# Weight-block sums on GpSimd in place of adding transfers, and two early products moved ahead of the last residual

## The chip, the core and the metric

The kernel runs on one core of a Trainium2 chip. The core has five engines that work side by side: TensorE (PE, matrix products; its weight loads are listed apart as PEld), VectorE (DVE), ScalarE (ACT), GpSimd (POOL) and SyncE (SP, which here only issues transfers). Sixteen DMA engines move data between the chip's memory and the core's SBUF. The metric is the time of one execution in microseconds on the device, as the median of several runs; lower is better.

## The reference

One block of a diffusion backbone: a token mixer (gated DeltaNet, short convolution and Fourier mixing, merged by gates, then an output projection w_o) and a SwiGLU sub-layer, on 512 latent tokens of 1024 channels, all in float32. The change lies where the mixer's output projection ends and the SwiGLU's first matrix begins:

```python
x = x + g1 * mix                                   # mix = merged @ w_o
h = modulate(x, norm2_g[layer], sh2, sc2)          # RMS norm, scale, shift
a, b = split_cols(h @ w_ffn_in[layer], (D_FF, D_FF))   # D_FF = 2816
x = x + g2 * ((jax.nn.silu(a) * b) @ w_ffn_out[layer])
return rmsnorm(x, final_g)
```

## The kernel before

**Precision.** Each float32 operand is split into a rounded high part and the remainder (`split`: ACT casts the high part, L143, then DVE subtracts, L144), and a product is made of three matmuls: high x high, high x low, low x high. `prep_w` does this for weights, into two rotating buffer pairs wh/wl, or into the pair that it is given as dst.

**The output projection.** `gemm_tm` keeps eight PSUM banks (four token blocks m of 128, two halves of 512 columns) and runs over the eight row blocks of w_o; the last four, whose split weights all lie ready, are run block by block of tokens, so that the blocks end one after another. After each m the loop adds the residual (`residual`, L1008: DVE adds, ACT squares), norms it into xn, transposes it on PE (L1071) and writes h in transposed form, scaled and shifted.

**Seven products in place of eight.** h is cut in halves by channels and by tokens, and w_ffn_in into 11 column blocks g of 256, each for a and b, each cut into halves by rows. For every g a scheme with sums of blocks needs seven products of 24 matmuls (`prod`, L1108). The token sides are called B11, B21 (tokens of m = 0, 1), nB22, T1, T2, T3 (which need m = 2, 3; `sums_b` makes them) and T4. The weight sides are: v = the a-block's upper half (with B11), a12 = its lower half (with B21; these two make X, the value of a for the first 256 tokens), t = the b-block's upper plus lower half (with T1), t + v (with T2), t + v + a12 (with nB22), w = v plus the b-block's upper half (with T3), and the b-block's lower half itself (with T4).

**Early products.** B11 and B21 are done before m = 2 and 3 are, so for the first three g (`EARLY`) the products with B11 (`ahead`) and B21 (`ahead2`) are run ahead of the loop over g. In the code they stand behind the whole projection loop; `ahead` also copies the first half's sum out of PSUM (e1s).

**The sums of weights.** t and w are made by transfers: SP loads one block into t (or w) and a transfer issued by POOL adds the other to it in SBUF (`acc_w`, L1113). DVE adds v and then a12 to t (`add_w`, L1117). t lies in two buffers at the end of the tile c16 (`pre`), which are free early, w in two tiles ws. The tiles of the pool pG (ws, the third pair of split weights, T4) lie where the projection's tiles were, so nothing can be written there before those are no longer used.

**What sets the order.** A scheduler puts the instructions of each engine, and of each DMA queue, into one fixed order, by priorities: what is issued under `prio("prep")` (loads, splits and sums of weights) goes ahead of the rest as far as its model thinks it ready. Each engine then runs its list in order and waits by semaphores. SP's list of transfers is such a list too: a load that waits for a buffer holds up all loads behind it. The loads go to a pool of three buffers wf.

Of the kernel before, what the change touches and what calls it, by code (L numbers as in the profile page):

```python
# [74 lines left out]
def body(tc, I, out):  # L75
# [3 lines left out]
    with es:  # L79
# [14 lines left out]
        @contextmanager  # L94
        def prio(name):
            save = tc.cur_priority
            tc.cur_priority = prios[name]
            yield
            prios[name] = tc.cur_priority
            tc.cur_priority = save  # L100
# [874 lines left out]
        def gemm_tm(w, scale, lhs, kt, extra=(), held=2):  # L975

            ps = [[((gbank if m < 3 else tbank) if n == 0 else dbank)() for n in range(2)] for m in range(4)]

            last = held + len(extra)

            def one(k, m, wh, wl, nn=(0, 1)):
                ms = slice(128 * m, 128 * m + 128)
                for n in nn:
                    ns = slice(512 * n, 512 * n + 512)
                    mm3(ps[m][n], *lhs(k, ms), wh[:, ns], wl[:, ns], k == 0, k == kt - 1)

            for k in range(kt - last):
                wt = load_rows(w[128 * k:128 * k + 128, :], scale)
                for m in range(4):
                    one(k, m, *wt)  # L990
            dsts = list(extra) + [None] * held
            tail = [(k, load_rows(w[128 * k:128 * k + 128, :], scale, dsts[i])) for i, k in enumerate(range(kt - last, kt))]
            for m in range(4):
                for n in range(2):
                    for k, wt in tail:
                        one(k, m, *wt, nn=(n,))
                yield m, ps[m]
# [4 lines left out]
        def residual(ps, xr, m, junk):  # L1002

            sm_ = const.tile([128, 2], F32, name="n_s", tag="n_s", bufs=2)
            rs_ = const.tile([128, 1], F32, name="n_r", tag="n_r", bufs=2)
            for n in range(2):
                ns = slice(512 * n, 512 * n + 512)
                V.tensor_tensor(out=xr[:, m, ns], in0=xr[:, m, ns], in1=ps[n], op=ALU.add)  # L1008
                A.activation(out=junk[n], in_=xr[:, m, ns], func=AF.Square, accum_out=sm_[:, n:n + 1])
            V.tensor_tensor(out=rs_, in0=sm_[:, 0:1], in1=sm_[:, 1:2], op=ALU.add)  # L1010
            A.activation(out=rs_, in_=rs_, func=AF.Sqrt, scale=1.0 / 1024, bias=eps)
            V.reciprocal(out=rs_, in_=rs_)
            return rs_
# [18 lines left out]
        pre = [c16[:, a:a + 1024].rearrange("p (k j) -> p k j", k=4) for a in (2048, 3072)]  # L1032
        OB = {"B11": ob[0][:, 0], "B21": ob[0][:, 1], "nB22": ob[1][:, 0], "T3": ob[1][:, 1], "T1": ob[2][:, 0], "T2": ob[2][:, 1]}

        def split_b(f, name, js):
            split(f, OB[name][:, 0, :, js], OB[name][:, 1, :, js])

# [19 lines left out]
                                       op1=ALU.subtract)  # L1057

        for m, ps in gemm_tm(I["w_o"][0], g1b, lambda k, ms: (mh[:, k, ms], ml[:, k, ms]), 8, extra, 1):
            rs_ = residual(ps, xr, m, [xn[:, m % 2, 512 * n:512 * n + 512] for n in range(2)])  # L1060
            V.tensor_scalar(out=xn[:, m % 2], in0=xr[:, m], scalar1=rs_, scalar2=None, op0=ALU.mult)
            js = slice(128 * (m % 2), 128 * (m % 2) + 128)
            hs = []
            for k4 in range(2):
                px = dbank()
                p3 = px.rearrange("p (k j) -> p k j", k=4)
                h3 = Bf[:, 4 * k4:4 * k4 + 4, js] if m < 2 else pF.tile([128, 512], F32, name="h2f", tag=("u", "gt")[m - 2], bufs=2).rearrange("p (k j) -> p k j", k=4)
                hs.append(h3)
                for kk in range(4):
                    k = 4 * k4 + kk  # L1070
                    T.transpose(p3[:, kk], xn[:, m % 2, 128 * k:128 * k + 128], ident)  # L1071
                for kk in range(4):
                    k = 4 * k4 + kk
                    if kk % 2:
                        A.activation(out=h3[:, kk], in_=p3[:, kk], func=AF.Identity, scale=a2[:, k:k + 1], bias=sh2[:, k:k + 1])
                    else:
                        V.tensor_scalar(out=h3[:, kk], in0=p3[:, kk], scalar1=a2[:, k:k + 1], scalar2=sh2[:, k:k + 1], op0=ALU.mult, op1=ALU.add)
                if m < 2:
                    split_b(h3, ("B11", "B21")[k4], js)
            if m == 2:  # L1080
                hs2 = hs
            elif m == 3:
                sums_b(((hs2, slice(0, 128)), (hs, slice(128, 256))))
# [8 lines left out]
        e1g, e5, u2, e57, c22, c21, c12 = (tmps[:, i] for i in range(7))  # L1092
        Gq = [pG.tile([128, 2, 512], F32, name="Gq", tag=f"Gq{i}") for i in range(11)]
        ws = [pG.tile([128, 4, 256], F32, name="ws", tag=f"ws{i}") for i in range(2)]
        third = [pG.tile([128, 4, 256], F32R, name="w3", tag=f"w3{i}") for i in range(2)]
        turn = itertools.count()
        prep3 = lambda w_: prep_w(w_, dst=third if next(turn) % 3 == 2 else None)
        wfi = I["w_ffn_in"][0].rearrange("(k p) f -> p k f", p=128)
        wsrc = lambda i, half, g: wfi[:, 4 * half:4 * half + 4, 2816 * i + 256 * g:2816 * i + 256 * g + 256]

        def prod(bank, w, b, first, last):

            for q in range(2):
                o, cs = bank[:, 256 * q:256 * q + 256], slice(128 * q, 128 * q + 128)
                for kk in range(4):
                    mm = ((w[0], b[:, 0]), (w[0], b[:, 1]), (w[1], b[:, 0]))
                    for i, (l_, r_) in enumerate(mm):
                        T.matmul(o, lhsT=l_[:, kk, cs], rhs=r_[:, kk], start=first and q == kk == i == 0,  # L1108
                                 stop=last and kk == 3 and i == 2, skip_group_check=True)

        def acc_w(w, src):
            with prio("prep"):
                GP.dma_start(out=w, in_=src, accum_op=ALU.add)  # L1113

        def add_w(w, other):
            with prio("prep"):
                V.tensor_tensor(out=w, in0=w, in1=other, op=ALU.add)  # L1117

        def load_w2(src, w):
            with prio("prep"):  # L1120
                SY.dma_start(out=w, in_=src)
            return w

        def ahead(g, e):

            X = gbank()
            prod(X, prep_w(load_w(wsrc(0, 0, g))), OB["B11"], True, False)
            A.copy(out=e, in_=X)
            return X

        def ahead2(g, X):
            prod(X, prep_w(load_w(wsrc(0, 1, g))), OB["B21"], False, True)
# [1 line left out]
        e01 = stg.tile([128, 4, 256], F32, name="e01", tag="wf", bufs=3).rearrange("p a b -> p (a b)")  # L1134
        e1s = [e01[:, 0:512], e01[:, 512:1024], e1g]
        EARLY = 3
        Xs = [ahead(g, e1s[g]) for g in range(EARLY)]
        for g in range(EARLY):
            ahead2(g, Xs[g])
        V.tensor_tensor(out=Bf[:, 4:8], in0=Bf[:, 4:8], in1=Bf[:, 0:4], op=ALU.subtract)  # L1140
# [2 lines left out]
        for g in range(EARLY):  # L1143
            A.activation(out=Gq[g][:, :, 0:256], in_=q2(Xs[g]), func=AF.Silu)
        for g in range(11):
            t, w = pre[g % 2], ws[g % 2]
            load_w2(wsrc(1, 0, g), t)
            acc_w(t, wsrc(1, 1, g))
            load_w2(wsrc(0, 0, g), w)
            acc_w(w, wsrc(1, 0, g))  # L1150
            v = load_w(wsrc(0, 0, g))
            if g < EARLY:
                e1 = e1s[g]
            else:
                X, e1 = gbank(), e1g
                prod(X, prep3(v), OB["B11"], True, False)
                A.copy(out=e1, in_=X)
            bA = gbank()
            prod(bA, prep3(t), OB["T1"], True, False)
            A.copy(out=e5, in_=bA)  # L1160
            add_w(t, v)
            bD = dbank()
            prod(bD, prep3(t), OB["T2"], True, True)
            V.tensor_tensor(out=u2, in0=bD, in1=e1, op=ALU.subtract)
            bB = gbank()
            prod(bB, prep3(w), OB["T3"], True, False)
            V.tensor_tensor(out=e57, in0=bB, in1=e5, op=ALU.add)
            V.tensor_tensor(out=c22, in0=u2, in1=e57, op=ALU.add)
            a12 = load_w(wsrc(0, 1, g))
            if g >= EARLY:  # L1170
                prod(X, prep3(a12), OB["B21"], False, True)
                A.activation(out=Gq[g][:, :, 0:256], in_=q2(X), func=AF.Silu)
            add_w(t, a12)
            prod(bA, prep3(t), OB["nB22"], False, True)
            V.tensor_tensor(out=c12, in0=u2, in1=bA, op=ALU.add)
            A.activation(out=Gq[g][:, :, 256:512], in_=q2(c12), func=AF.Silu, scale=-1.0)
            prod(bB, prep3(load_w(wsrc(1, 1, g))), OB["T4"], False, True)
            V.tensor_tensor(out=c21, in0=u2, in1=bB, op=ALU.add)
            for c_, cs in ((c22, slice(256, 512)), (c21, slice(0, 256))):
                V.tensor_tensor(out=Gq[g][:, :, cs], in0=q2(c_), in1=Gq[g][:, :, cs], op=ALU.mult)  # L1180
# [38 lines left out]
```

## Time and profile before

| | us |
|---|---|
| median of 3 runs (963.09 to 968.24) | 963.99 |
| the profiled execution's own time | 965.04 |
| its span in the profile | 963.2 |
| PE busy | 939.9 |
| DVE busy | 649.3 |
| ACT busy | 467.9 |
| POOL busy | 57.2 |

The page lists the busy time of each engine, then groups of instructions as "line engine operation out<-in count, busy time, mean of one in ns, idle time before them and what ended it". A row of the timeline gives the start and the length in us, then engine, line, operation, tiles and count, and in brackets how long the engine had been idle and which instruction released it. "SPq" is SP's queue of transfers. A row of stretches gives, for each engine, its busy us and instructions, then the granted TensorE clock (1.00 is full), the mean busy share of the DMA engines and the GB/s. A row of the chain of waits gives start, length, engine, line and count.

### The profile page before, as it was taken

To read this page: it belongs to the slowest core of one execution; us is meant where nothing else is said; L and a number is where in the kernel's file an instruction comes from. 1 tells how busy PE (TensorE), PEld (TensorE's weight loads), DVE (VectorE), ACT (ScalarE), POOL (GpSimd) and SP (SyncE) were. 2 spreads that over 40 slices of the span, in tenths; PEclk is the share of its full clock that TensorE was granted. 3 is DMA by queue.
4 is the path that set the end of the run, shared out by engine and by line. 5 is a ranking of instruction groups with operands and counts; after the bars stand their busy time and mean duration, and the time that the engine had idled before them with its cause. 6 is when DMAs were issued, how large, how long until landed. Compare 5 with 4: busy or idle time off the path is not lost.

```text
span 963.2 us, 16357 instructions
## 1 busy us (share of the span) xinstructions
PE 939.9 (98%) x6660; PEld 807.7 (84%) x6660; DVE 649.3 (67%) x1002; ACT 467.9 (49%) x793; POOL 57.2 (6%) x69
## 2 busy tenths in 40 slices
PE   8999999999999999999999999799999999999997
PEld 7588887777788888888888888699999999988885
DVE  2585888378755423788874876778777777855575
ACT  5354885687673334362234336644444444422334
POOL 1002300000000000000000010112111110000000
PEclk9999999999999999999999999899999999999999
DMA  9920653521202232837774471689887774333332
GB/s 319 307 66 3 146 131 88 133 67 34 67 2 66 88 110 66 310 109 256 264 247 141 127 194 42 160 217 262 180 195 190 185 187 104 117 88 109 89 88 87
DMA packets 117434, 135.84 MB, mean 141 GB/s; under 512 B 18748, under 2 KB 104624, under 8 KB 117360
## 3 DMA queue, kind: packets, MB, share of 16 engines
q1 hardware_dynamic: 97168, 117.93, 39.2%
q0 software_dynamic: 13248, 14.98, 9.5%
q10 hardware_dynamic: 6944, 1.91, 0.8%
q8 instruction: 52, 0.85, 0.4%
q14 instruction: 22, 0.18, 0.1%
HBM read 131.02 MB, written 3.77 MB: 140 GB/s over the span
## 4 chain that ended last, share of the span: by engine, by line
PE 76%; DVE 9%; DMA 6%; ACT 6%; issue 2%; POOL 0%; SPq 0%; DVEq 0%; ACTq 0%
PE g L1108 17%; PE g L256 10%; PE g L257 10%; PE g L255 10%; PE d L256 5%; PE d L255 5%; PE d L257 5%; PE d L1108 3%; DVE wl L144 2%; DMA wm<-in_w_mod_dram 2%; DMA ws<-in_w_ffn_in_dram 1%; DVE acc L835 1%; DMA wf<-in_w_o_dram 1%; ACT wh L143 1%; ACT SJ L718 1%
## 5 line engine op out<-in xcount | busy, mean ns | idle before, releaser
L144 DVE TENSOR_TENSOR wl<-wf,wh 128x1024 fp32r<-128x1024 f32 x114 | 139.1, 1222 | 93.1 <-ACT wh L143 92.2
L143 ACT CAST wh<-wf 128x1024 fp32r<-128x1024 f32 x114 | 119.6, 1050 | 161.1 <-PE g L256 98.2
L255 PE MATMUL g<-hh,wh 128*128 128x512 f32 x368 | 145.6, 396 | 0.0
L257 PE MATMUL g<-hh,wl 128*128 128x512 f32 x368 | 145.3, 395 | 0.1
L256 PE MATMUL g<-hl,wh 128*128 128x512 f32 x368 | 145.2, 395 | 0.0
L1108 PE MATMUL g<-ob,wh 128*128 128x256 f32 x640 | 118.7, 287 | 3.8 <-ACT wh L143 3.8
L1108 PEld LDWEIGHTS g<-ob,wh 128*128 128x128 f32 x640 | 101.6, 195 | 4.5 <-ACT wh L143 4.5
L1108 PE MATMUL g<-ob,wl 128*128 128x256 f32 x320 | 91.6, 287 | 0.5 <-DVE wl L144 0.5
L257 PEld LDWEIGHTS g<-hh,wl 128*128 128x128 f32 x368 | 69.2, 188 | 14.5 <-issue 0.5
L256 PEld LDWEIGHTS g<-hl,wh 128*128 128x128 f32 x368 | 69.2, 188 | 13.6 <-issue 0.2
L255 PEld LDWEIGHTS g<-hh,wh 128*128 128x128 f32 x368 | 69.2, 188 | 13.6 <-issue 0.2
L1108 PEld LDWEIGHTS g<-ob,wl 128*128 128x128 f32 x320 | 62.3, 195 | 0.8 <-DVE wl L144 0.8
L835 DVE SCALAR_TENSOR_TENSOR acc<-wm,ct,acc 128x1024 f32<-128x1024 f32 x32 | 41.0, 1282 | 14.7 <-DMA acc<-in_b_mod_dram 7.6
L1108 PE MATMUL g<-ob,w 128*128 128x256 f32 x360 | 45.9, 283 | 0.2 <-issue 0.2
L1108 PEld LDWEIGHTS g<-ob,w 128*128 128x128 f32 x360 | 44.3, 192 | 0.4 <-issue 0.4
L143 ACT CAST gs<-Gq 128x512 fp32r<-128x512 f32 x22 | 13.4, 622 | 63.5 <-PE d L256 63.5
L143 ACT CAST wh<-c 128x1024 fp32r<-128x1024 f32 x21 | 22.0, 1048 | 37.0 <-DVE c L1117 19.5
L144 DVE TENSOR_TENSOR gs<-Gq,gs 128x512 fp32r<-128x512 f32 x22 | 15.0, 690 | 29.1 <-ACT gs L143 29.1
L154 DVE TENSOR_TENSOR wf<-wf,g2b 128x1024 f32<-128x1024 f32 x22 | 26.9, 1222 | 8.5 <-DMA wf<-in_w_ffn_out_dram 8.5
L255 PE MATMUL d<-wh,gs 128*128 128x512 f32 x80 | 31.1, 389 | 0.0
L257 PE MATMUL d<-wh,gs 128*128 128x512 f32 x80 | 31.1, 389 | 0.0
L256 PE MATMUL d<-wl,gs 128*128 128x512 f32 x80 | 31.1, 389 | 0.0
(481 smaller groups left out, 2078.3 us busy)
## 6 DMA issues: line engine op xcount, KB each, us to landing
wm<-in_w_mod_dram SPq DMA_DIRECT2D x48, 512.0 KB, 5.7
wf<-in_w_ffn_in_dram SPq DMA_DIRECT2D x39, 512.0 KB, 4.8
wf<-in_w_in_dram SPq DMA_DIRECT2D x31, 512.0 KB, 3.8
wf<-in_w_gate_dram SPq DMA_DIRECT2D x24, 512.0 KB, 3.8
wf<-in_w_ffn_out_dram SPq DMA_DIRECT2D x22, 512.0 KB, 3.6
c<-in_w_ffn_in_dram SPq DMA_DIRECT2D x11, 512.0 KB, 6.3
c<-in_w_ffn_in_dram POOLq DMA_DIRECT2D x11, 512.0 KB, 6.6
ws<-in_w_ffn_in_dram SPq DMA_DIRECT2D x11, 512.0 KB, 3.8
```

The lines of the kernel that those rows point to most:

```text
L143: A.copy(out=hi, in_=f)
L144: V.tensor_tensor(out=lo, in0=f, in1=hi.bitcast(F32), op=ALU.subtract)
L154: V.tensor_tensor(out=w, in0=w, in1=scale, op=ALU.mult)
L255: T.matmul(ps, lhsT=lh, rhs=rh, start=start, stop=False)
L256: T.matmul(ps, lhsT=lh, rhs=rl, start=False, stop=False)
L257: T.matmul(ps, lhsT=ll, rhs=rh, start=False, stop=stop)
L718: A.activation(out=S[:, u ^ par, h], in_=S[:, u ^ par, h], func=AF.Copy, scale=eGl[:, u, c_:c_ + 1])
L835: V.scalar_tensor_tensor(out=acc, in0=w, scalar=ct[:, k, 0:1], in1=acc, op0=ALU.mult, op1=ALU.add)
L1108: T.matmul(o, lhsT=l_[:, kk, cs], rhs=r_[:, kk], start=first and q == kk == i == 0, stop=last and kk == 3 and i == 2, skip_group_check=True)
```

## The change

`prod`, `wfi` and `wsrc` are moved up unchanged. Inside the projection's loop, at m = 3 and ahead of that block's residual, the products of g = 0 and 1 with B11 are now issued; the split weights of g = 1 go into the place of nB22, which is filled later. The copies to e1s and the third early product stay behind the loop. A further tile low (one of its own, two in c16's first half) holds the b-block's lower half, which also serves the T4 product, so it is loaded once. ws holds the b-block's upper half; GpSimd writes t = ws + low, then w = ws + v in place.

```diff
         for m, ps in gemm_tm(I["w_o"][0], g1b, lambda k, ms: (mh[:, k, ms], ml[:, k, ms]), 8, extra, 1):
+            if m == 3:
+
+                Xs = [gbank() for _ in range(2)]
+                for g, dst in enumerate((None, (OB["nB22"][:, 0], OB["nB22"][:, 1]))):
+                    prod(Xs[g], prep_w(load_w(wsrc(0, 0, g)), dst=dst), OB["B11"], True, False)
             rs_ = residual(ps, xr, m, [xn[:, m % 2, 512 * n:512 * n + 512] for n in range(2)])
...
+        low = [pG.tile([128, 4, 256], F32, name="low", tag="low")]
+        low += [c16[:, a:a + 1024].rearrange("p (k j) -> p k j", k=4) for a in (0, 1024)]
...
-        def acc_w(w, src):
+        def sum_w(out, a, b, eng):
             with prio("prep"):
-                GP.dma_start(out=w, in_=src, accum_op=ALU.add)
-
-        def add_w(w, other):
-            with prio("prep"):
-                V.tensor_tensor(out=w, in0=w, in1=other, op=ALU.add)
+                eng.tensor_tensor(out=out, in0=a, in1=b, op=ALU.add)
...
-        Xs = [ahead(g, e1s[g]) for g in range(EARLY)]
+        for g in range(2):
+            A.copy(out=e1s[g], in_=Xs[g])
+        Xs.append(gbank())
+        prod(Xs[2], prep_w(load_w(wsrc(0, 0, 2))), OB["B11"], True, False)
+        A.copy(out=e1s[2], in_=Xs[2])
...
-            t, w = pre[g % 2], ws[g % 2]
-            load_w2(wsrc(1, 0, g), t)
-            acc_w(t, wsrc(1, 1, g))
-            load_w2(wsrc(0, 0, g), w)
-            acc_w(w, wsrc(1, 0, g))
+            t, w, a22 = pre[g % 2], ws[g % 2], low[g % 3]
+            load_w2(wsrc(1, 0, g), w)
+            load_w2(wsrc(1, 1, g), a22)
             v = load_w(wsrc(0, 0, g))
+            sum_w(t, w, a22, GP)
+            sum_w(w, w, v, GP)
...
-            add_w(t, v)
+            sum_w(t, t, v, V)
...
-            add_w(t, a12)
+            sum_w(t, t, a12, V)
             prod(bA, prep3(t), OB["nB22"], False, True)
...
-            prod(bB, prep3(load_w(wsrc(1, 1, g))), OB["T4"], False, True)
+            prod(bB, prep3(a22), OB["T4"], False, True)
```

On PE, at the end of the projection, before: the first early product (PSUM bank g_5735, weights wh_5738 and wl_5739), the transposes of m = 3 (from xn), then the second (g_5767).

```order
L1108 MATMUL g_5735<-ob_5311,wh_5738 128x256 x2
L1108 MATMUL g_5735<-ob_5311,wl_5739 128x256
L1071 MATMUL d_5669<-cp_82,xn_5310 128x128 x4
L1071 MATMUL d_5679<-cp_82,xn_5310 128x128 x4
L1108 MATMUL g_5767<-ob_5311,wh_5770 128x256 x2
L1108 MATMUL g_5767<-ob_5311,wl_5771 128x256
```

And at the same place now, with the second product's split weights in ob_5312 (nB22):

```order
L1045 MATMUL g_5659<-ob_5311,wh_5663 128x256 x2
L1045 MATMUL g_5659<-ob_5311,wl_5664 128x256
L1045 MATMUL g_5660<-ob_5311,ob_5312 128x256 x24
L1089 MATMUL d_5729<-cp_82,xn_5310 128x128 x4
L1089 MATMUL d_5739<-cp_82,xn_5310 128x128 x4
L1045 MATMUL g_5798<-ob_5311,wh_5801 128x256 x2
L1045 MATMUL g_5798<-ob_5311,wl_5802 128x256
```

The second product's 24 matmuls have moved from behind the transposes to ahead of them; the third (g_5798) now follows the transposes directly.

On SP's queue from the last w_o loads on, before: the two loads of t for g = 0 and 1 (c16) stand ahead of four w_o loads, and the first two of w (ws) behind five loads for early products.

```order
L139 DMA wf_5416<-in_w_o_dram 128x1024
L1121 DMA c16_5314<-in_w_ffn_in_dram 128x4x256 x2
L139 DMA wf_5447<-in_w_o_dram 128x1024
L139 DMA wf_5452<-in_w_o_dram 128x1024
L139 DMA wf_5457<-in_w_o_dram 128x1024
L139 DMA wf_5462<-in_w_o_dram 128x1024
L139 DMA wf_5736<-in_w_ffn_in_dram 128x4x256
L139 DMA wf_5768<-in_w_ffn_in_dram 128x4x256
L139 DMA wf_5800<-in_w_ffn_in_dram 128x4x256
L139 DMA wf_5831<-in_w_ffn_in_dram 128x4x256
L139 DMA wf_5861<-in_w_ffn_in_dram 128x4x256
L1121 DMA ws_5730<-in_w_ffn_in_dram 128x4x256
```

Now, from the last w_o load on:

```order
L139 DMA wf_5462<-in_w_o_dram 128x1024
L139 DMA wf_5661<-in_w_ffn_in_dram 128x4x256
L139 DMA wf_5691<-in_w_ffn_in_dram 128x4x256
L139 DMA wf_5799<-in_w_ffn_in_dram 128x4x256
L139 DMA wf_5830<-in_w_ffn_in_dram 128x4x256
L139 DMA wf_5860<-in_w_ffn_in_dram 128x4x256
L139 DMA wf_5890<-in_w_ffn_in_dram 128x4x256
L139 DMA wf_5928<-in_w_ffn_in_dram 128x4x256
L1125 DMA ws_5790<-in_w_ffn_in_dram 128x4x256
L1125 DMA low_5792<-in_w_ffn_in_dram 128x4x256
L139 DMA wf_6022<-in_w_ffn_in_dram 128x4x256
L1125 DMA ws_5791<-in_w_ffn_in_dram 128x4x256
```

The loads of t are gone from ahead of the w_o loads; the first two blocks that t is made of (ws_5790, low_5792) stand behind six loads for early products and the load of v (wf_5928). By the semaphores of this list, wf_5860 waits for the split of wf_5799, wf_5928 for the split of wf_5860, and ws_5790 for DVE's last subtraction in `sums_b`.

On POOL's queue behind the last small transfer of the mixer, before:

```order
L830 DMA acc_4842<-in_b_mod_dram 1x16x64
L1113 DMA c16_5314<-in_w_ffn_in_dram 128x4x256 x2
L1113 DMA ws_5730<-in_w_ffn_in_dram 128x4x256
L1113 DMA ws_5731<-in_w_ffn_in_dram 128x4x256
L1113 DMA ws_5730<-in_w_ffn_in_dram 128x4x256
```

and now:

```order
L830 DMA acc_4842<-in_b_mod_dram 1x16x64
L1121 ISA
L1121 TENSOR_TENSOR c16_5314<-ws_5790,low_5792 128x1024
L1121 TENSOR_TENSOR ws_5790<-ws_5790,wf_5928 128x1024
L1121 TENSOR_TENSOR c16_5314<-ws_5791,c16_5314 128x1024
L1121 TENSOR_TENSOR ws_5791<-ws_5791,wf_6088 128x1024
```

The adding transfers are replaced by additions on GpSimd itself, two per g, t first; ahead of them stands one instruction (ISA) that reloads the engine's code library and waits for no semaphore.

More of the change, by code (lines that the diff above doesn't have):

```diff
@@ L1033, in body, with prod @@
         OB = {"B11": ob[0][:, 0], "B21": ob[0][:, 1], "nB22": ob[1][:, 0], "T3": ob[1][:, 1], "T1": ob[2][:, 0], "T2": ob[2][:, 1]}
+        wfi = I["w_ffn_in"][0].rearrange("(k p) f -> p k f", p=128)
+        wsrc = lambda i, half, g: wfi[:, 4 * half:4 * half + 4, 2816 * i + 256 * g:2816 * i + 256 * g + 256]
+        def prod(bank, w, b, first, last):
+            for q in range(2):
+                o, cs = bank[:, 256 * q:256 * q + 256], slice(128 * q, 128 * q + 128)
+                for kk in range(4):
+                    mm = ((w[0], b[:, 0]), (w[0], b[:, 1]), (w[1], b[:, 0]))
+                    for i, (l_, r_) in enumerate(mm):
+                        T.matmul(o, lhsT=l_[:, kk, cs], rhs=r_[:, kk], start=first and q == kk == i == 0,
+                                 stop=last and kk == 3 and i == 2, skip_group_check=True)
         def split_b(f, name, js):
@@ L1097, in body @@
         prep3 = lambda w_: prep_w(w_, dst=third if next(turn) % 3 == 2 else None)
[L1098 to L1109, printed above, removed]
-        def acc_w(w, src):
+        def sum_w(out, a, b, eng):
             with prio("prep"):
-                GP.dma_start(out=w, in_=src, accum_op=ALU.add)
-        def add_w(w, other):
-            with prio("prep"):
-                V.tensor_tensor(out=w, in0=w, in1=other, op=ALU.add)
+                eng.tensor_tensor(out=out, in0=a, in1=b, op=ALU.add)
         def load_w2(src, w):
@@ L1122, in load_w2 @@
             return w
[L1124 to L1129, printed above, removed]
         def ahead2(g, X):
```

## The prediction

> **What bounds the kernel now.** I read the busy shares first, then who TensorE (PE) waits for from 560 us on, then PE's timeline at those waits, then the chain of waits.
>
> ```profile
> PE   939.9 (98%) x6660; PEld 807.7 (84%) x6660; DVE 649.3 (67%) x1002; ACT 467.9 (49%) x793; POOL 57.2 (6%) x69
> PE g L1108 <- ACT wh L143: 4.3, 4, 2.1
> PE d L1071 <- DVE xn L1061: 1.2, 1, 1.2
> PE d L1108 <- ACT wh L143: 1.0, 1, 1.0
> PE g L1108 <- DVE wl L144: 0.5, 1, 0.5
> 682.73 17.28 PE g L1108 x144
> ```
>
> PE is busy for 98% of the span, and later in the product loop 144 products' matmuls run in 17.28 us without a gap, 0.12 us each: a product of 24 takes 2.88 us, and nothing but less PE work could shorten that stretch. What an order of work can win lies in the change-over from the output projection to the products:
>
> ```profile
> 599.26 0.40 PE L1108 MATMUL g<-ob,wh 128*128 128x256 f32 x2
> ...
> 603.54 1.06 PE L1071 MATMUL d<-cp,xn 128*128 128x128 f32 x8 [1.25 <-DVE xn L1061]
> 606.74 0.80 PE L1108 MATMUL g<-ob,wh 128*128 128x256 f32 x2 [2.14 <-ACT wh L143]
> 608.00 0.58 PE L1108 MATMUL g<-ob,wl 128*128 128x256 f32 x1 [0.46 <-DVE wl L144]
> 608.38 0.63 PE L1108 MATMUL g<-ob,wh 128*128 128x256 f32 x2
> ...
> 612.23 0.50 PE L1108 MATMUL g<-ob,wh 128*128 128x256 f32 x2
> ...
> 624.36 0.51 PE L1108 MATMUL g<-obt,wh 128*128 128x256 f32 x2 [0.44 <-ACT wh L143]
> ...
> 639.36 0.40 PE L1108 MATMUL g<-ob,wh 128*128 128x256 f32 x2
> 605.00:610.00 5.00, 2.79 (x11) 2.50 (x12) 4.75 (x8) 4.37 (x8) 0.00 (x0) 0.56 0.15 39
> 630.00:635.00 5.00, 3.69 (x19) 3.10 (x19) 2.63 (x4) 2.57 (x3) 1.27 (x1) 0.79 0.71 225
> ```
>
> From 599.26 (projection done) to 639.36 (block 0's nB22 product) PE does nine products and eight transposes: 9 x 2.88 + 1.06 = 27.0 us of work in 40.1 us. So **13.1 us** are lost there, the ceiling for this part. Some are waits; some are slow matmuls: between 608.38 and 612.23 eighteen matmuls take 3.85 us, 0.214 each and not 0.12, 1.7 us too much, and the granted clock in that stretch's row is 0.56 (third field from its end). A second slow stretch shows as 0.79. Each follows waits of PE.
>
> **The change, part by part.**
>
> *Products X0 and X1 ahead of the last residual.* PE now runs both from 599.26 to 605.0 (48 x 0.12), then the eight transposes without their 1.25 us wait, since xn was ready at 603.5; one more split (1.22) ahead of it on DVE makes that 604.7, still in time. The third product X2 then waits. ACT may write the negated B22 piece only when X1 has read its weights there, and the cast for X2 is queued behind it.
>
> ```profile
> 599.99 0.63 ACT L1055 ACTIVATE ob<-h2f 128x512 fp32r<-128x512 f32 x1
> 602.36 0.57 ACT L1128 COPY e<-g 128x512 f32<-128x512 f32 x1
> L143 ACT CAST wh<-wf 128x1024 fp32r<-128x1024 f32 x114 | 119.6, 1050 | 161.1 <-PE g L256 98.2
> L144 DVE TENSOR_TENSOR wl<-wf,wh 128x1024 fp32r<-128x1024 f32 x114 | 139.1, 1222 | 93.1 <-ACT wh L143 92.2
> ```
>
> 605.1 + 0.63 + 0.57 + 1.05 = 607.4 for the cast, 608.6 for the low part: 0.6 us later than the second product stood (608.00), with one product of 2.88 more done. **Lead 2.3 us**, X2 done at 611.3.
>
> *What is late next: block 0's sums.* Before, t of blocks 0 and 1 was loaded and summed by DMA long ahead, into c16. Now its two loads need memory that frees when DVE has finished the last B sums, and on SP they stand behind the loads for the early products and for v. A load takes this long:
>
> ```profile
> 614.84 0.92 SPq L1121 DMA_DIRECT2D ws<-in_w_ffn_in_dram  x2
> 619.50 2.58 POOL L1113 DMA_DIRECT2D ws<-in_w_ffn_in_dram  x2 [60.39 <-DMA ws<-in_w_ffn_in_dram]
> 617.00 8.02 SPq L139 DMA_DIRECT2D wf<-in_w_ffn_in_dram  x3
> 622.32 1.05 ACT L143 CAST wh<-wf 128x1024 fp32r<-128x1024 f32 x1 [1.76 <-DMA wf<-in_w_ffn_in_dram]
> ```
>
> That is 4.7 and 5.3 us. X2's split at 608.6 frees the buffer for the second B21 weights: landed 613.3, cast 614.3, split 615.5; this releases v's load at 615.5, then ws at 615.9 and low at 616.3, which lands at 621.3, with SP's a12 and next ws behind it. PE meanwhile runs the three B21 products, the second held for 615.5, and is through at 621.1.
>
> *GpSimd's adds.* Two per block, 22 in all, in place of 22 adding transfers. No row shows GpSimd reading two operands; the nearest is its own memset of the same 128x1024, one stream:
>
> ```profile
> L829 POOL MEMSET acc<- 128x1024 f32 x4 | 3.8, 954 | 238.4 <-ACT merged L805 149.6 <-DVE at L850 58.6 <-DVE as L144 30.2
> L1113 POOL DMA_DIRECT2D ws<-in_w_ffn_in_dram x11 | 14.1, 1304 | 160.1 <-DMA ws<-in_w_ffn_in_dram 150.8 <-issue 9.3
> ```
>
> An add moves three streams, so it takes 0.95 us if they overlap and 2.86 one after another; if it also waits out one DVE instruction first, 2.86 + 1.22 = 4.1. I take 2.86, the same engine's rate. The Trainium skill's GPSIMD Engine Reference, section Performance versus the Vector engine, has 4497 ns for 2048 elements, so 2.25 us here as an estimate; no run here shows it, and by it the forecast below would be 1.2 us lower.
>
> With 2.86: t at 624.2, cast 625.2, so T1's first two matmuls start at 625.2, 0.8 **later** than now (624.36). PE's order puts two of T3 next; their w is summed after t: 627.0, cast 628.1, split 629.3. So PE idles nearly from 621.1 to 628.1, then does 22 of T1 and 6 of T3 (3.4 us), with one slow stretch of +1.7 as above: 633.2. DVE adds v (630.5), cast 631.6, split 632.8; T2 and T3's rest are 40 matmuls, 4.8 us: nB22 starts at **638.0, against 639.36: -1.4 us**. Each microsecond of an add counts twice here. At 0.95 us nB22 starts at 634.2 (-5.2), at 4.1 at 640.5 (+1.1).
>
> *The rest of the loop.* Seven 512 KB transfers per block become four, and the adding rows on POOL (1.30 each) go. PE does not wait there now, so that wins nothing until the loop's end. Two other waits go by the way:
>
> ```profile
> 568.86 0.50 PE L256 MATMUL g<-wl,mh 128*128 128x512 f32 x1 [0.27 <-DVE wl L144]
> 836.45 0.50 PE L256 MATMUL g<-wl,gs 128*128 128x512 f32 x1 [0.61 <-DVE wl L144]
> ```
>
> The first came from w_o loads that shared the DMA engines with the early sums, the second from a w_ffn_out load queued behind loop loads: **-0.9 us**, bounds 0 and -0.9. The library instruction ahead of the first add waits for nothing but POOL's row before it:
>
> ```profile
> 480.17 0.49 POOL L830 DMA_DIRECT2D acc<-in_b_mod_dram  x1 [0.29 <-POOL acc L829]
> ```
>
> From there to 621.3 POOL has 140 us for it; its length no row shows, and without that cover it would come on top of t.
>
> *X1's weights* are split on DVE ahead of the first residual:
>
> ```profile
> 566.44 1.23 DVE L154 TENSOR_TENSOR wf<-wf,g1b 128x1024 f32<-128x1024 f32 x1 [3.04 <-DMA wf<-in_w_o_dram]
> 573.79 1.22 DVE L144 TENSOR_TENSOR ex<-wf,ex 128x1024 fp32r<-128x1024 f32 x1
> 577.34 0.68 DVE L1008 TENSOR_TENSOR xr<-xr,g 128x512 f32<-128x512 f32 x1
> 579.88 0.69 DVE L1008 TENSOR_TENSOR xr<-xr,d 128x512 f32<-128x512 f32 x1 [1.86 <-PE d L257]
> ```
>
> Their load waits for the split that ends at 575.0; ahead of it DVE waited 3.04 us for a w_o load that ran beside the early sums' transfers. With most of that gone, I put the end at 572.3, and 572.3 + 4.7 + 1.05 + 1.22 = 579.3. The first half of the residual slips by 2, its second half, which counts, stands at 579.9: no cost. From 575.0 it would be 582.0, 2.1 us of delay.
>
> **The sum.** -1.4 - 0.9 = -2.3 us from the profiled run's own 965.04 (span 963.2 and 1.84 around it): 962.7. The median of the three runs, 963.99, is 1.05 lower; by it, 961.7. I write 962.0.
>
> **The rivals.**
>
> *Cheap adds, no slow stretch (faster).* With adds of 0.95 to 1.9 us and the clock kept: -5.2 to -3.3, -1.7, -0.9, so -7.8 to -5.9: 957 to 959. For it: PE then waits only some 3 to 5 us. Against it: waits of 3.85 us around 603 to 608 did bring the slow stretch.
>
> *GpSimd's adds hold up DVE (slower).* In the loop the low half of T2's weights is ready just ahead of PE:
>
> ```profile
> 736.89 1.22 DVE L144 TENSOR_TENSOR w<-c,w 128x1024 fp32r<-128x1024 f32 x1
> 740.16 2.08 PE L1108 MATMUL d<-obt,w 128*128 128x256 f32 x16
> 700.00:720.00 20.00, 20.00 (x169) 20.00 (x168) 15.16 (x17) 9.31 (x11) 2.59 (x2) 1.00 0.86 208
> ```
>
> Ready at 738.1, used at 740.16: 2.0 us in hand. An add that stops DVE for longer than 2.0 us makes PE wait for the rest: 2.86 - 2.0 = 0.9 us, in blocks 1 to 10 some 9 us, so 962 + 9 = 971; if half of them meet a DVE gap, 966.5. It decides from a hold of 2.0 us. Against it: DVE has 4.8 us free in 20 (15.16 busy), the two adds need 5.7, and four of DVE's operations per block read PSUM. The memsets show no such hold, but they read nothing. The Trainium skill speaks for it: SBUF — State Buffer (its shared-port rules) says that a DVE operation with two SBUF inputs and a GpSimd operation that reads SBUF exclude each other for a whole instruction. Splits and adds on DVE are of that kind. No run here shows it yet.
>
> *The products move, but nothing is won.* X1's weights come late (582.0) or loads take 1 us longer with three in flight: the gap before T1 eats the lead, 964 to 965.
>
> **How the numbers follow.** Forecast (960 to 964) 0.40; cheap and unslowed 0.27; nothing won 0.13; DVE held up 0.20. What a measurement of this kernel can tell from no change is about 0.5%, 4.8 us: below 959.2 is faster, above 968.8 slower. Faster takes the cheap case, 0.27; slower most of the held-up case and a little of unknown loads, 0.18; same 0.55. The range reaches from the middle of the cheap case, 957.5, to the middle of the held-up one, 969.0.
>
> **What would show it.** PE's timeline: X0 and X1 in one run from 599, then transposes without a wait; X2 held for ACT and DVE to about 608.6; a gap of 5 to 7 us before T1 and T3, released by GpSimd's sums; nB22 near 638. GpSimd's add near 2.9 us a row. Of the rivals: no granted clock below 0.9 around 625 to 635; or PE waits on DVE's wl spread over blocks 1 to 10, with DVE operations stretched or late beside GpSimd's. The forecast fails if an add takes far from 2.9 us or low lands far from 621.

## The result and the profile after

| | before | after |
|---|---|---|
| median, us (4 runs each, taken together) | 963.54 (962.31 to 968.24) | 974.8 (973.58 to 976.01) |
| the profiled execution's own time | 965.04 | 974.27 |
| its span | 963.2 | 972.5 |
| DVE busy | 649.3 | 684.1 |
| POOL busy | 57.2 | 86.3 |

The ratio of the times is 1.0101, with a 95% interval of 1.0065 to 1.0137: **the change makes the kernel 1% slower**. First the busy times of the page and the list of who PE waits for, from 560 us on (total us, number of waits, longest). The waits come to some 16 us; before, they were 8.

```profile
PE 941.0 (97%) x6660; PEld 807.0 (83%) x6660; DVE 684.1 (70%) x1002; ACT 469.3 (48%) x793; POOL 86.3 (9%) x69
PE g L1045 <- ACT wh L143: 5.7, 2, 4.9
PE g L1045 <- DVE wl L144: 3.7, 5, 1.4
PE g L1045 <- ACT w L143: 1.6, 1, 1.6
PE g L1045 <- DVE w L144: 1.6, 1, 1.6
PE d L1045 <- DVE w L144: 1.6, 2, 0.8
PE g L1045 <- DVE tmps L1168: 1.4, 1, 1.4
```

Next PE's timeline of after at the places that the prediction named, and the start of the next stage (L255) and the last store (ACTq):

```profile
600.62 0.40 PE L1045 MATMUL g<-ob,wh 128*128 128x256 f32 x2
...
606.38 1.03 PE L1089 MATMUL d<-cp,xn 128*128 128x128 f32 x8
608.16 0.50 PE L1045 MATMUL g<-ob,wh 128*128 128x256 f32 x2 [0.75 <-ACT wh L143]
609.42 0.39 PE L1045 MATMUL g<-ob,wl 128*128 128x256 f32 x1 [0.76 <-DVE wl L144]
...
626.02 0.79 PE L1045 MATMUL g<-obt,wh 128*128 128x256 f32 x2 [4.92 <-ACT wh L143]
628.46 0.79 PE L1045 MATMUL g<-ob,w 128*128 128x256 f32 x2 [1.64 <-ACT w L143]
...
639.20 0.40 PE L1045 MATMUL g<-ob,wh 128*128 128x256 f32 x2
641.03 0.38 PE L1045 MATMUL g<-ob,wl 128*128 128x256 f32 x1 [1.44 <-DVE wl L144]
...
845.63 0.40 PE L255 MATMUL g<-wh,gs 128*128 128x512 f32 x1
...
969.16 0.34 ACTq L1208 DMA_DIRECT2D out_dram<-yos  x1
```

And of before, the last two of these:

```profile
835.20 0.40 PE L255 MATMUL g<-wh,gs 128*128 128x512 f32 x1
...
959.60 0.34 ACTq L1207 DMA_DIRECT2D out_dram<-yos  x1
```

With the two starts of before that the prediction shows (599.26 and 639.36), the difference falls into four parts:

| stretch | before, us | after, us | difference | the prediction |
|---|---|---|---|---|
| up to the first early product | 599.26 | 600.62 | +1.36 | -0.3 |
| change-over, to block 0's nB22 | 40.10 | 38.58 | **-1.52** | -1.4 |
| the rest of the loop, to the next stage | 195.84 | 206.43 | **+10.59** | 0 |
| from there to the last store | 124.40 | 123.53 | -0.87 | -0.6 |

The whole loss lies in the third row. It holds eight PE waits, from 641.03 to 701.32, which add up to 7.41 us, all on DVE. The other 3.2 us stand in no wait row; 2.3 of them show in the window below, where 428 matmuls take 53.62 us and not 51.4 (0.12 each): the rows at a wait are longer, as at 641.03, where the next matmul starts after 0.23 us. Behind 701.32 PE does not wait there any more. Nothing shows the +1.36 to be an effect of the change: in the profiles of after and of three runs below that differ from it only in the sums (on DVE, memsets, copies), the first early product starts anywhere between 598.73 and 601.90 us.

What holds DVE is seen when its rows in after are laid beside GpSimd's (first DVE, then POOL):

```profile
626.00 2.40 DVE L144 TENSOR_TENSOR wl<-c,wh 128x1024 fp32r<-128x1024 f32 x1 [3.66 <-ACT wh L143]
...
637.67 3.31 DVE L144 TENSOR_TENSOR wl<-c,wh 128x1024 fp32r<-128x1024 f32 x1 [1.17 <-ACT wh L143]
640.90 0.68 DVE L1165 TENSOR_TENSOR tmps<-d,e 128x512 f32<-128x512 f32 x1
641.51 3.04 DVE L144 TENSOR_TENSOR wl<-low,wh 128x1024 fp32r<-128x1024 f32 x1
644.47 1.21 DVE L144 TENSOR_TENSOR w<-c,w 128x1024 fp32r<-128x1024 f32 x1
```

```profile
627.27 3.36 POOL L1121 TENSOR_TENSOR c<-ws,c 128x1024 f32<-128x1024 f32 x1
637.51 2.39 POOL L1121 TENSOR_TENSOR ws<-ws,wf 128x1024 f32<-128x1024 f32 x1 [6.88 <-DMA wf<-in_w_ffn_in_dram]
641.06 2.40 POOL L1121 TENSOR_TENSOR c<-ws,c 128x1024 f32<-128x1024 f32 x1 [1.16 <-DVE wl L144]
```

A GpSimd add runs from 637.51 to 639.90. DVE's subtraction that starts at 637.67 has the same shape as the one at 644.47, but takes 3.31 us and not 1.21: about what is left of the add, 2.2, and then its own time. The next pair, at 641.06 and 641.51, does the same, and so it goes on:

```profile
651.69 3.43 DVE L1121 TENSOR_TENSOR c<-c,wf 128x1024 f32<-128x1024 f32 x1
661.72 2.90 DVE L1169 TENSOR_TENSOR tmps<-tmps 128x512 f32<-128x512 f32 x1
```

From 641 to 701 us eight of DVE's rows last 2.46 to 3.43 us where they otherwise take 1.22 (128x1024) or 0.69 (128x512). That is 15.9 us more, 1.98 for each of GpSimd's eight adds there. The hold goes the other way too: the add at 627.27 takes 3.36 us, as DVE's instruction of 626.00 was at work until 628.40. PE's wait at 641.03 is for the first of these subtractions.

Two windows tell where this costs something. Of after, first 640 to 700, then a piece of the later loop:

```profile
640.00:700.00 60.00, 53.62 (x428) 51.96 (x429) 58.20 (x49) 22.14 (x26) 21.15 (x8) 1.00 0.37 115
720.00:740.00 20.00, 20.00 (x168) 19.97 (x167) 18.00 (x17) 9.21 (x12) 4.90 (x3) 1.00 0.34 106
```

And of before, 640 to 700:

```profile
640.00:700.00 60.00, 60.00 (x503) 60.00 (x502) 51.06 (x56) 26.56 (x32) 8.96 (x7) 1.00 0.91 222
```

The third pair of figures behind the length is DVE. From 640 to 700 it is busy for 58.20 of 60 us (51.06 before): DVE, not PE, sets the pace there. From 720 on DVE has 18.00 of 20 us to do (15.16 before, in the prediction's row), and PE works on without a gap.

### The profile page after: what moved, and what is told of

Its sections match the earlier page's. It is cut to its first block, busy times and chain, and to the rows that moved or that the text cites. A ratio compares the mean times of both kernels' runs of the same rounds, so it can differ in the third digit from the quotient of the medians.

```text
span 972.5 us, 16344 instructions
## 1 busy us (share of the span) xinstructions
PE 941.0 (97%) x6660; PEld 807.0 (83%) x6660; DVE 684.1 (70%) x1002; ACT 469.3 (48%) x793; POOL 86.3 (9%) x69
## 4 chain that ended last, share of the span: by engine, by line
PE 75%; DVE 10%; ACT 5%; DMA 5%; issue 3%; POOL 1%; SPq 0%; DVEq 0%; ACTq 0%; POOLq 0%
PE g L1045 15%; PE g L255 10%; PE g L256 10%; PE g L257 10%; PE d L255 5%; PE d L256 5%; PE d L257 5%; DVE wl L144 4%; PE d L1045 3%; DMA wm<-in_w_mod_dram 2%; DVE acc L835 1%; PE t L257 1%; PE t L256 1%; PE t L255 1%; ACT SJ L718 1%
## 5 line engine op out<-in xcount | busy, mean ns | idle before, releaser
L144 DVE TENSOR_TENSOR wl<-wf,wh 128x1024 fp32r<-128x1024 f32 x105 | 130.4, 1242 | 81.7 <-ACT wh L143 80.7
L143 ACT CAST wh<-wf 128x1024 fp32r<-128x1024 f32 x105 | 110.3, 1051 | 151.5 <-PE g L256 99.0
L255 PE MATMUL g<-hh,wh 128*128 128x512 f32 x368 | 146.1, 397 | 0.0
L1045 PE MATMUL g<-ob,wh 128*128 128x256 f32 x624 | 113.8, 283 | 2.1 <-DVE tmps L1168 1.4
L1045 PEld LDWEIGHTS g<-ob,wh 128*128 128x128 f32 x624 | 97.3, 192 | 2.7 <-issue 1.5
L1045 PE MATMUL g<-ob,wl 128*128 128x256 f32 x312 | 89.1, 285 | 2.8 <-DVE wl L144 2.8
L255 PEld LDWEIGHTS g<-hh,wh 128*128 128x128 f32 x368 | 69.5, 189 | 13.5 <-issue 0.2
L1045 PEld LDWEIGHTS g<-ob,wl 128*128 128x128 f32 x312 | 59.8, 192 | 3.7 <-DVE wl L144 3.4
L143 ACT CAST wh<-c 128x1024 fp32r<-128x1024 f32 x25 | 26.2, 1049 | 48.2 <-DVE c L1121 27.2
L144 DVE TENSOR_TENSOR wl<-c,wh 128x1024 fp32r<-128x1024 f32 x25 | 41.6, 1664 | 7.6 <-ACT wh L143 7.6
L1121 POOL TENSOR_TENSOR ws<-ws,wf 128x1024 f32<-128x1024 f32 x11 | 29.7, 2696 | 16.9 <-DMA wf<-in_w_ffn_in_dram 16.3
L255 PE MATMUL d<-wh,gs 128*128 128x512 f32 x80 | 31.1, 389 | 0.0
```

Of the source, the lines that this page charges most:

```text
L143: A.copy(out=hi, in_=f)
L144: V.tensor_tensor(out=lo, in0=f, in1=hi.bitcast(F32), op=ALU.subtract)
L255: T.matmul(ps, lhsT=lh, rhs=rh, start=start, stop=False)
L1121: eng.tensor_tensor(out=out, in0=a, in1=b, op=ALU.add)
```

## The experiments

Three theories were put against each other. **A:** GpSimd's adds and DVE's instructions with two SBUF operands exclude each other, and DVE has no time to spare in the first blocks. **B:** the loads are late, since t of blocks 0 and 1 is not in memory ahead of the loop any more. **C:** the early products' splits put DVE behind at the change-over, and it stays behind. All times are medians with the lowest and highest run; the ratio is to the kernel before on the same chip. The diffs are against the changed kernel, where nothing else is said; "..." stands for lines left out.

### GpSimd writes, but hardly reads

```diff
-                eng.tensor_tensor(out=out, in0=a, in1=b, op=ALU.add)
+                if eng is V:
+                    V.tensor_tensor(out=out, in0=a, in1=b, op=ALU.add)
+                else:
+                    GP.tensor_tensor(out=out[:, 0:1, 0:8], in0=a[:, 0:1, 0:8], in1=b[:, 0:1, 0:8], op=ALU.add)
+                    GP.memset(out, 0.01)
+                    GP.memset(out[:, 0:2], 0.02)
+                    GP.memset(out[:, 2:4], 0.03)
```

> The changed kernel with each GpSimd add replaced by an add over 8 of 1024 columns (so that it waits for the same two loads) and memsets of the whole and of two halves, together about 2.1 to 2.4 us on GpSimd: the same order, the same loads, about the same GpSimd time, but it reads next to nothing. t and w hold constants, so the products of T1, T2, T3 and nB22 are not the reference's. Theory A: DVE's split rows stand at 1.22 us beside them, DVE's busy total falls to about 650, the PE waits behind 640 us (7.4 us in the changed kernel) fall under 2 us, time 961 to 966. Theory B and C: unchanged, 973 to 976.

Measured: 963.62 us (962.1 to 964.95, 10 runs), ratio 0.999 (0.9976 to 1.0004), as theory A expected. The group of DVE's splits out of c16 (t and its sums, mostly), the loop's last wait of PE and two windows of this kernel:

```profile
L144 DVE TENSOR_TENSOR wl<-c,wh 128x1024 fp32r<-128x1024 f32 x25 | 30.6, 1223 | 10.7 <-ACT wh L143 10.7
628.58 0.80 PE L1045 MATMUL g<-obt,wh 128*128 128x256 f32 x2 [6.19 <-ACT wh L143]
640.00:700.00 60.00, 60.00 (x503) 60.00 (x502) 50.98 (x56) 26.86 (x31) 15.49 (x28) 1.00 0.43 132
740.00:760.00 20.00, 20.00 (x169) 20.00 (x169) 15.18 (x17) 9.35 (x11) 4.64 (x8) 1.00 0.34 106
```

The order, the loads and the waits for them are those of the changed kernel, and T1 of block 0 waits even longer for its weights, 6.19 us. Still 11.2 us are gone. These splits stand at 1223 ns (1664 in after), DVE's busy total at 649.9, and PE works through 640 to 700. So the loss does not come from the late loads (B) or the early products (C) by themselves, which are all still there; it comes with GpSimd's reading.

### The sums on DVE

```diff
-            sum_w(t, w, a22, GP)
-            sum_w(w, w, v, GP)
+            sum_w(t, w, a22, V)
+            sum_w(w, w, v, V)
```

> The changed kernel with its two sums per block on DVE in place of GpSimd; nothing else differs. Theory A (a GpSimd add and a DVE instruction with two SBUF operands exclude each other, so an add costs DVE 1.2 to 2.2 us although DVE does not compute it): DVE's rows stand at 1.22 us, its busy total is about 649 + 22 x 1.22 = 676 us, not above the changed kernel's 684, t and w of block 0 come 1.1 us earlier each, and the time is 966 to 973. Theory B (the loss comes from the loads: t of blocks 0 and 1 is no longer in memory ahead of the loop, whoever adds): the loads are as late as before, DVE has more to do, time 974 to 980. Theory C (the early products' two extra splits put DVE behind by some us at the change-over and it never catches up): 974 to 980 as well.

Measured: 964.89 us (962.87 to 967.65, 10 runs), ratio 1.0005 (0.9986 to 1.0024), 1 us under A's range and far from that of B and C. DVE's busy total is 672.4, 23.1 above before for 22 adds: 1.05 us each. With the adds on GpSimd it was 684.1, 34.8 above before: **1.58 us of DVE's time for each add that DVE did not do**. Behind 640 us PE waits three times, 2.0 us in all.

### Each part alone

Early products alone: the changed kernel, with the loop's sums put back, and with them the second load of the b-block's lower half for the T4 product.

```diff
-            load_w2(wsrc(1, 0, g), w)
-            load_w2(wsrc(1, 1, g), a22)
+            load_w2(wsrc(1, 0, g), t)
+            acc_w(t, wsrc(1, 1, g))
+            load_w2(wsrc(0, 0, g), w)
+            acc_w(w, wsrc(1, 0, g))
             v = load_w(wsrc(0, 0, g))
-            sum_w(t, w, a22, GP)
-            sum_w(w, w, v, GP)
...
-            prod(bB, prep3(a22), OB["T4"], False, True)
+            prod(bB, prep3(load_w(wsrc(1, 1, g))), OB["T4"], False, True)
```

> The early products moved ahead of the last residual as in the changed kernel, but the weight-block sums by adding transfers as before, t of blocks 0 and 1 loaded ahead. Theory A: nothing holds DVE, PE waits little behind 640 us: 957 to 962. Theory B: the preloaded t is back: 957 to 962 as well. Theory C: the loss stays, above 968.

Measured: 962.11 us (960.75 to 966.97, 10 runs), ratio 0.9987 (0.9971 to 1.0002). GpSimd's sums alone, with the three early products behind the projection:

```diff
-            if m == 3:
-                Xs = [gbank() for _ in range(2)]
...
-        for g in range(2):
-            A.copy(out=e1s[g], in_=Xs[g])
+        Xs = []
+        for g in range(EARLY):
+            Xs.append(gbank())
+            prod(Xs[g], prep_w(load_w(wsrc(0, 0, g))), OB["B11"], True, False)
+            A.copy(out=e1s[g], in_=Xs[g])
...
```

> GpSimd's sums alone; all three early products stand behind the projection as before. Theory A and B: the loss stays, 972 to 979 (the change-over does not get its 1.5 us). Theory C: the loss goes, 962 to 966.

Measured: 971.97 us (971.2 to 974.12, 4 runs), ratio 1.0086 (1.0065 to 1.0106). The loss goes with the sums, and C falls. The moved products win nothing that their interval shows; the one large wait left there is in the section on the faster version.

### t of blocks 0 and 1 loaded ahead again

```diff
+            if g < 2:
+                load_w2(wsrc(1, 0, g), t)
+                acc_w(t, wsrc(1, 1, g))
...
-            sum_w(t, w, a22, GP)
+            if g >= 2:
+                sum_w(t, w, a22, GP)
             sum_w(w, w, v, GP)
```

> The changed kernel, but t of blocks 0 and 1 loaded and added by transfers ahead of the loop as before; the other 20 sums stay on GpSimd. Theory A: the 4.9 us wait for T1 of block 0 goes, but DVE is still held in blocks 0 to 4, and PE, being ahead, waits there for what it won: 968 to 973. Theory B (late loads are the loss): 960 to 964.

Measured: 969.76 us (969.06 to 972.02, 6 runs), ratio 1.0058 (1.0038 to 1.0078). This lies in A's range. The gap of 4.92 us ahead of T1 is gone, and still more than half of the loss stays, with PE waits on DVE from 653 to 697 us. So B falls a second time, though not without a share: with the adds on GpSimd, the missing preload costs some 5 us (974.8 to 969.76).

### Which blocks pay

GpSimd sums blocks 5 to 10 and adding transfers the first five; then the other way round (the condition turned to g >= 5).

```diff
+            if g < 5:
+                load_w2(wsrc(1, 0, g), t)
+                acc_w(t, wsrc(1, 1, g))
+                load_w2(wsrc(0, 0, g), w)
+                acc_w(w, wsrc(1, 0, g))
+                v = load_w(wsrc(0, 0, g))
+            else:
...
                 sum_w(t, w, a22, GP)
                 sum_w(w, w, v, GP)
...
```

> The early products moved; blocks 0 to 4 sum their weights by adding transfers, blocks 5 to 10 by GpSimd (12 adds). Theory A with its place (a steady block of seven products is 20.2 us of PE and about 15.3 of DVE; two adds cost DVE 2.4, so 17.7 still fits): split rows of 2 to 3.4 us beside the adds, DVE's busy share in 740 to 800 near 18 of 20, no PE wait there: 960 to 964, the same as with the early products alone. The prediction's rival as it was put (0.9 us lost in every block): 6 x 0.9 more, 965 to 969.

> The counterpart of the run with GpSimd's sums from block 5 on: the early products moved, GpSimd sums blocks 0 to 4 (10 adds), adding transfers sum blocks 5 to 10. If the loss sits where DVE has no time left (blocks 0 to 2 have five products, 14.4 us of PE, against about 12.9 of DVE), 10 adds lose what 22 do: 972 to 976, with PE's waits on DVE between 640 and 705. If it were spread over all blocks: 10 of 22 parts of the loss, 967 to 970.

Measured: GpSimd late 965.95 us (961.37 to 970.9, 10 runs), ratio 1.0023 (1.0002 to 1.0043); GpSimd early 973.93 us (971.23 to 978.54, 4 runs), ratio 1.0098 (1.0069 to 1.0127). Ten adds in the first five blocks cost as much as all 22 (1.0101), within the intervals. In the late version's profile, DVE is busy for 18.09 of 20 us in 760 to 780 and PE does not wait; in all its GpSimd blocks there is one wait:

```profile
728.03 2.89 PE L1045 MATMUL g<-ob,w 128*128 128x256 f32 x22 [0.55 <-DVE w L144]
760.00:780.00 20.00, 20.00 (x168) 19.97 (x167) 18.09 (x16) 9.23 (x11) 5.15 (x2) 1.00 0.34 102
```

Its median is a miss for theory A with its place, though: it lies 3.8 us above that of the early products alone, in the range that the prediction's rival gave (965 to 969), and its runs spread over 9.5 us. The profile is of its fastest run, so what the others lose stays open. What the pair does show is the place of most of the loss: ten early adds cost some 12 us against the early products alone, twelve late ones under 4.

### Five adds for one

Against the version with GpSimd's sums from block 5 on:

```diff
-                sum_w(t, w, a22, GP)
+                for _ in range(5):
+                    sum_w(t, w, a22, GP)
                 sum_w(w, w, v, GP)
```

> As the last, but in blocks 5 to 10 GpSimd does the first of its two adds five times (same operands, same result), so six adds per block, about 15 us of GpSimd's time in 20.2. Theory A: six adds cost DVE 6 x 1.2 = 7.3 us or more on top of 15.3, 22.6 against 20.2, so DVE bounds these blocks: 6 x 2.4 = 14 us lost, 974 to 985, with PE waits on DVE's splits in blocks 5 to 10. If an add only delays single instructions and DVE makes it up in its gaps: below 966.

Measured: 1012.68 us (1011.6 to 1014.25, 4 runs), ratio 1.0502 (1.0476 to 1.0528): A's direction, but 46.7 us above the version with one add and not 14. DVE's rows while GpSimd runs its five adds, and the five adds (the last row):

```profile
742.08 3.43 DVE L144 TENSOR_TENSOR w<-c,w 128x1024 fp32r<-128x1024 f32 x1
745.43 3.42 DVE L144 TENSOR_TENSOR wl<-wf,wh 128x1024 fp32r<-128x1024 f32 x1
748.77 0.68 DVE L1188 TENSOR_TENSOR tmps<-tmps,g 128x512 f32<-128x512 f32 x1
749.37 2.82 DVE L144 TENSOR_TENSOR wl<-c,wh 128x1024 fp32r<-128x1024 f32 x1
752.12 2.88 DVE L1193 TENSOR_TENSOR Gq<-tmps,Gq 128x512 f32<-128x512 f32 x1
...
739.20 15.25 POOL L1121 TENSOR_TENSOR c<-ws,c 128x1024 f32<-128x1024 f32 x5 [10.91 <-DVE wl L144]
```

The two engines take turns: each DVE instruction with two SBUF operands waits out one add. The one at 748.77, which reads one operand (g) from PSUM, takes its usual 0.68 us in the midst of them. DVE's busy total is 49.1 us above the late version's, 2.05 us for each of the 24 extra adds; A had taken 1.2. The five adds also end nearly 13 us later than one would, and t with them. PE's longest wait in each of the six blocks (4.3 us in five of them, 2.2 in the first, 24 in all) hangs on it: it is for the cast of what DVE adds to t, and that addition comes just behind the five adds and is then held by the next one.

```profile
754.93 3.36 DVE L1121 TENSOR_TENSOR c<-c,wf 128x1024 f32<-128x1024 f32 x1
759.49 0.79 PE L1045 MATMUL d<-obt,w 128*128 128x256 f32 x2 [4.36 <-ACT w L143]
```

So the run shows the hold clearly, but not what part of the 46.7 us is DVE's lack of time and what part is t's lateness.

### One operand read

```diff
-                eng.tensor_tensor(out=out, in0=a, in1=b, op=ALU.add)
+                if eng is V:
+                    V.tensor_tensor(out=out, in0=a, in1=b, op=ALU.add)
+                else:
+                    GP.tensor_tensor(out=out[:, 0:1, 0:8], in0=a[:, 0:1, 0:8], in1=b[:, 0:1, 0:8], op=ALU.add)
+                    GP.tensor_copy(out=out, in_=b)
```

> The changed kernel with each GpSimd add replaced by an add over 8 of 1024 columns (for the waits) and a GpSimd copy of one operand, full size: one stream read instead of two. t and w hold one addend, so the products of T1, T2, T3 and nB22 are not the reference's. If any GpSimd instruction that reads SBUF holds DVE's instructions with two SBUF operands: those rows again over 1.22 us by the length of the copy, DVE's busy total above 665, time 966 to 974. If only GpSimd instructions with two operands hold it: rows of 1.22, DVE near 650, 961 to 966 as with memsets.

Measured: 961.16 us (958.61 to 965.34, 10 runs), ratio 0.9973 (0.9954 to 0.9993). Two GpSimd copies, one undisturbed and one not, and DVE's split beside the first:

```profile
648.94 1.04 POOL L1125 COPY c<-low 128x1024 f32<-128x1024 f32 x1
653.64 2.04 POOL L1125 COPY ws<-wf 128x1024 f32<-128x1024 f32 x1
```

```profile
649.12 1.94 DVE L144 TENSOR_TENSOR wl<-c,wh 128x1024 fp32r<-128x1024 f32 x1
```

Neither expectation fits whole. A copy excludes DVE as well: 1.94 us in place of 1.22, and a copy 2.04 in place of 1.04. But it lasts only 1.04 us, DVE's busy total is 655.9, and behind 640 us PE does not wait in the loop. So reading one operand is enough for the hold; what it costs goes by how long the GpSimd instruction lasts.

### A faster version

With the early products alone, one large wait was left, for w of block 0, whose adding transfer lands late. PE's row names another load, but the weights that it needs are those that ACT casts from 626.29 on, when the adding transfer into ws has landed:

```profile
626.29 1.04 ACT L143 CAST w<-ws 128x1024 fp32r<-128x1024 f32 x1 [2.37 <-DMA ws<-in_w_ffn_in_dram]
627.44 0.77 PE L1045 MATMUL g<-ob,w 128*128 128x256 f32 x2 [2.96 <-DMA wf<-in_w_ffn_in_dram]
```

Against that version, block 0 takes its w from DVE:

```diff
+            if g < 1:
+                load_w2(wsrc(1, 0, g), w)
+                v = load_w(wsrc(0, 0, g))
+                sum_w(w, w, v, V)
+            else:
...
```

> The early products alone (adding transfers kept), but w of block 0 is summed by DVE from the two loads at hand, as its adding transfer lands only at 626.2 and PE waits 2.96 us for it. Expected: w cast at about 624 and not at 626.3, the wait at 627.4 gone or under 0.8, the slow clock behind it gone with it: 957.5 to 960, the fastest so far. If DVE's extra 1.22 us there pushes T2 of block 0 back by as much: 961 to 962.5, nothing won.

Measured: **958.28 us** (956.42 to 960.25, 6 runs), ratio 0.9937 (0.9915 to 0.996). The same place, in a run whose first early product starts 1.4 us later:

```profile
627.44 1.45 PE L1045 MATMUL g<-ob,w 128*128 128x256 f32 x10 [0.63 <-DVE w L144]
```

The slow matmuls behind the wait went with it: the granted clock from 625 to 635 us is 1.00 in this profile, where that of the early products alone has 0.63 and 0.69. One add by DVE, where DVE has time, wins more than 22 by GpSimd. This version is 0.6% faster than the kernel before, and faster than the changed one.

## Why the prediction was wrong

**The early products: right.** X0 and X1 ran in one stretch, the transposes followed without a wait, and the third product was held for ACT and DVE to 609.42, 608.1 without the 1.36 us; 608.6 was forecast.

**Block 0's sums and the slow clock: right.** T1 was forecast at 625.2 and T3 at 628.1; they came at 626.02 and 628.46, so 624.7 and 627.1 without the 1.36. The granted clock fell as forecast (third field from the end):

```profile
625.00:630.00 5.00, 2.34 (x9) 2.04 (x10) 3.97 (x2) 2.02 (x2) 5.00 (x2) 0.50 0.43 149
630.00:635.00 5.00, 5.00 (x31) 5.00 (x31) 3.83 (x3) 1.53 (x2) 0.63 (x1) 0.64 0.37 114
```

An undisturbed add takes 2.33 to 2.40 us, not 2.86, near the estimate from the Trainium skill's GPSIMD Engine Reference, section Performance versus the Vector engine (2.25). The change-over won 1.52 us against 1.4. That the whole comes so close is partly luck: two shorter adds brought T3 1.0 us earlier than forecast, and two holds of DVE that the forecast lacks, in the rows at 626.00 and 628.43 (1.2 and 2.1 us), used it up.

**The small waits: right.** No wait stands at 568 or behind the loop; the last stretch is 0.87 us shorter.

**The rest of the loop: the step that failed.** The forecast had the removed transfers "win nothing" there, and gave the new adds no price on DVE. The stretch got 10.6 us longer. The mechanism stood among the rivals, with a chance of 0.20, but its place and its test were wrong. It was put into blocks 1 to 10, at 0.9 us each, to be decided by whether one hold exceeds the 2.0 us that a split is ready ahead. In after, single holds of 2 us made no PE wait behind 701.32, since DVE makes them up in its gaps; only the median of the version with late adds, 3.8 us too high, leaves a share of the later blocks open. What decides is DVE's total per block. A full block has seven products, 20.2 us of PE, and 15.16 x 20.2 / 20 = 15.3 us of DVE; two adds at 1.58 us make 18.5, which fits. Blocks 0 to 2 have only five products, 14.4 us, and DVE saves but two splits there: 15.3 - 2.4 = 12.9 (in the profile of before, DVE is busy for 12.70 of the 14.4 us from 639.36 on). With two adds at 1.58 that is 16.1, so 1.7 us too many in each, 5.1 in three. But an add costs more where DVE is always busy: at the 1.98 us that the rows from 641 to 701 show, it is 2.5 in each, 7.4 in three. PE's waits came to 7.41. That this fits so well is in part chance: a piece of block 0 lies ahead of 641, and the last three waits (1.65 us in all) lie behind block 2, where DVE was presumably still behind. With DVE's own adds (1.05 us each) the same sum gives 0.6 x 3 = 1.8 us, and 2.0 were measured.

The argument against the rival, "DVE has 4.8 us free in 20", was weak by its own numbers, as two adds were put at 5.7 us, and it was read from a window of the later loop. The window from 640 to 700 of the same profile, with DVE at 51.06 of 60 us, would have shown the place where there was no such reserve. The Trainium skill's page SBUF — State Buffer (section Who interferes with whom) says that a DVE instruction with two SBUF inputs and a GpSimd instruction that reads SBUF exclude each other for a whole instruction, and one that only writes does not. The traces agree: 3.31 us beside an add, 1.94 beside a copy, 1.22 beside memsets. The DVE rows with one operand in PSUM kept their 0.68.

## What to carry to other kernels

An elementwise operation on SBUF that is given to GpSimd is not free for DVE: price it by the time for which it holds DVE's instructions with two SBUF operands, here 1.58 us for an add that DVE itself does in 1.05, and 1.98 where DVE had no gaps. Judge the room for it stage by stage, in the stage where the idle engine is least idle (here blocks with five products and not seven), and by the engine's total there, not by the lead of one instruction. Where a sum is late in one place, add it there on the engine that has time, and leave the other sums to the transfers.

## What the runs showed of the hardware

Work taken off an engine can cost it more than doing it: 22 adds on GpSimd put 34.8 us on DVE's busy total, on DVE itself 23.1. The exclusion is mutual and by whole instructions: GpSimd's add stretches from 2.33 to 3.36 us, its copy from 1.04 to 2.04. When both have work, they alternate, one instruction each, as in the run with five adds (15.25 us for five). A slow stretch of PE's clock followed a wait and went with it: 0.63 and 0.69 behind a wait of 2.96 us, 1.00 where that wait was 0.63 us.
